# Head norms rewritten by algebra, the MLP's row norm moved to its second product, and a new TensorE order ahead of the attention

## The chip, the cores and the metric

The kernel runs on one core of one Trainium2 chip. The metric is the device time of one execution in microseconds (us), the median of the runs of a kernel. Inside the core the engines run side by side, each through its own list of instructions in order: TensorE (PE, the matmuls), VectorE (DVE), ScalarE (ACT), GpSimd (POOL) and SyncE (SP), which here only issues the transfers (DMA).

## What is computed

Two decoder layers over 256 tokens of 1024 numbers, all in 32-bit floats. The first layer mixes by two attentions (latent attention with compressed queries and keys, and a dilated one); the second by a causal block attention. Each then has a squared-ReLU MLP and a gated input embedding.

```python
def rms_norm(x, g):
    return x * lax.rsqrt(jnp.mean(x * x, axis=-1, keepdims=True) + EPS) * g

for i in range(DEPTH):
    hn = rms_norm(h, mix_norm[i])
    # layer 0: z = hn @ w_in; c_q, c_kv = rms_norm of columns of z (384 and 256 wide);
    #   q = c_q @ w_uq, kv = c_kv @ w_ukv; norms of each head of q and k; rotary parts; attention;
    #   dilated q, k (normed by head), v = other columns of z; attention; both @ w_out
    # layer 1: q, k, v = hn @ w_in; norms of each head of q and k; attention; @ w_out
    h = h + mix
    u = jax.nn.relu(rms_norm(h, ff_norm[i]) @ w_ff1[i])
    h = h + (u * u) @ w_ff2[i]
    g = jax.nn.sigmoid(rms_norm(h, ple_norm[i]) @ w_ple_gate[i])
    h = h + g * (p[i] @ w_ple_proj[i])
```

## The kernel before

**Products in three passes.** Each float32 operand is split into a rounded part `hi` (ACT, line 107) and the rest `lo` (DVE, line 108), and a product is the sum hi·hi + hi·lo + lo·hi. A weight chunk is 1 MB in the big stages and is split in four pieces of 128x512 numbers, so each chunk costs ACT four `hi` and DVE four `lo`. Activations `x` are kept with `hi` and `lo` side by side, so that one matmul of 512 columns (line 233) and one of 256 (line 235) do a chunk's three passes in the MLP.

**Norms.** The gain of a layer's norm is put into `x`; the factor of a row, `rsqrt(mean)`, is applied to a product after the matmul. `Norm.square` sums the squares on ACT and DVE into `acc`; `Norm.rows` (a factor for each token on a partition, two columns) and `Norm.cols` (the same factors along the free axis, 128x256) make TensorE add them over the partitions (tile `st`, lines 195 and 206) and take the root with `rsqrt` (lines 86 to 99): a logarithm and an exponential on ACT and a Newton step of four DVE instructions. `heads_norm` (279), `mla_queries` (680), `mla_keys` (708) and `compress` (646) do the norm of heads and latents with the same `rsqrt`; the squares there wait for the row factor `r`, since the product is scaled by it on the way. The normed tile `z` is then transposed by TensorE (`tr`, line 273).

**MLP.** `up` takes 16 chunks of the first weight: two outputs `f` in the two PSUM banks of pool `pa`, which ACT and DVE add together (lines 490 and 491), DVE clips and multiplies by the row factor (line 492), ACT squares (494) and splits (495, 496). `down` takes 16 chunks of the second weight, and DVE adds the two halves of its product to `h` (507, 508). `cols` of the MLP is called after the first of chunk 0's two outputs.

**What sets the order.** In the stages of attention and projection TensorE's order is that of the code (`manual_schedule`); the very first block, with the combined latent projection (`w_c`, 416 columns in 8 pieces, and `w_kv`), has the order of the code on all engines. Elsewhere, the MLP and the gate included, a scheduler orders the instructions. `take` issues the transfers and splits of weight chunks two chunks ahead. The dense products come in units of six matmuls (`tok_units`), and the attention of four pairs of heads lays units between scores, transposes and values (`attention`, its list `units` saying how many). ACT, DVE and SP take weight splits, norms and softmax in one list each, so a small step waits behind the pieces that stand ahead of it.

## Time and profile before

| | us |
|---|---|
| runs: median of 3 | 697.8 |
| lowest, highest run | 694.3, 698.08 |
| the profiled execution | 692.53 |
| its span (what the profile shows) | 690.5 |
| TensorE busy | 662.8 |
| VectorE busy | 535.4 |
| ScalarE busy | 432.4 |
| GpSimd busy | 7.7 |

The profile shows one execution: for each instruction the engine, the line of the kernel, start and length, and, where an engine stood idle, what released it. `out<-in` are tile names. Matmuls overlap, so the lengths of single ones add up to more than the time that they take: 0.39 us of a 512-column matmul stand 0.23 us apart. A wait stands in brackets behind the instruction that ended it. The granted clock is that of TensorE: 1.00 is its level of 2.4 GHz, and a stretch at 0.50 ran at the lower one, 1.2 GHz.

### The profile page before, as it was taken

To read this page: it belongs to the slowest core of one execution; us is meant where nothing else is said; L and a number is where in the kernel's file an instruction comes from. 1 tells how busy PE (TensorE), PEld (TensorE's weight loads), DVE (VectorE), ACT (ScalarE), POOL (GpSimd) and SP (SyncE) were. 2 spreads that over 40 slices of the span, in tenths; PEclk is the share of its full clock that TensorE was granted. 3 is DMA by queue.
4 is the path that set the end of the run, shared out by engine and by line. 5 is a ranking of instruction groups with operands and counts; after the bars stand their busy time and mean duration, and the time that the engine had idled before them with its cause. 6 is when DMAs were issued, how large, how long until landed. Compare 5 with 4: busy or idle time off the path is not lost.

```text
span 690.5 us, 10700 instructions
## 1 busy us (share of the span) xinstructions
PE 662.8 (96%) x3862; PEld 566.8 (82%) x3862; DVE 535.4 (78%) x1335; ACT 432.4 (63%) x996; POOL 7.7 (1%) x28
## 2 busy tenths in 40 slices
PE   8988999989999999999997999999899999999996
PEld 7776888968888888888876777888788888888885
DVE  5699768688877877879995687666788778787896
ACT  6877786567745647446873676766577465573572
POOL 3100000000000000000000000000000000000000
PEclk9999999999999999999999999999899999999999
DMA  7555433154555555555444443331555655555411
GB/s 231 235 191 181 193 123 123 62 183 158 190 203 183 184 183 183 183 184 183 149 166 173 161 144 137 123 123 61 186 188 193 216 185 192 183 183 187 179 62 61
DMA packets 19492, 114.07 MB, mean 165 GB/s; under 512 B 2288, under 2 KB 5488, under 8 KB 6640
## 3 DMA queue, kind: packets, MB, share of 16 engines
q1 hardware_dynamic: 19440, 113.40, 46.5%
q8 instruction: 30, 0.49, 0.3%
q14 instruction: 22, 0.18, 0.1%
HBM read 112.34 MB, written 1.05 MB: 164 GB/s over the span
## 4 chain that ended last, share of the span: by engine, by line
PE 84%; DVE 6%; ACT 5%; DMA 3%; issue 1%; SPq 1%; POOL 0%; ACTq 0%; DVEq 0%
PE f L233 34%; PE f L235 17%; PE mm L251 12%; PE mm L220 7%; PE g L233 4%; ACT hi L107 3%; PE g L235 2%; DVE lo L108 2%; DMA raw<-w_dil 2%; PE tr L349 1%; PE tr L273 1%; PE s L318 1%; PE o L358 1%; PE s L316 1%; DMA raw<-w_c 1%
## 5 line engine op out<-in xcount | busy, mean ns | idle before, releaser
L107 ACT ACTIVATE hi<-raw 128x512 fp32r<-128x512 f32 (+2 forms) x418 | 237.7, 623 | 121.4 <-PE f L233 82.5
L108 DVE TENSOR_TENSOR lo<-raw,hi 128x512 fp32r<-128x512 f32 (+2 forms) x418 | 270.6, 686 | 37.8 <-ACT hi L107 36.9
L233 PE MATMUL f<-x,hi 128*128 128x512 f32 x512 | 183.8, 403 | 5.8 <-ACT hi L107 5.8
L233 PE MATMUL f<-u,hi 128*128 128x512 f32 x512 | 179.5, 396 | 0.0
L235 PE MATMUL f<-x,lo 128*128 128x256 f32 x512 | 144.7, 283 | 0.0
L235 PE MATMUL f<-u,lo 128*128 128x256 f32 x512 | 142.8, 279 | 0.0
L233 PEld LDWEIGHTS f<-x,hi 128*128 128x128 f32 x512 | 98.1, 192 | 30.2 <-ACT hi L107 6.6
L233 PEld LDWEIGHTS f<-u,hi 128*128 128x128 f32 x512 | 96.1, 188 | 23.1
L251 PE MATMUL mm<-hi,x 128*128 128x512 f32 (+1 forms) x320 | 107.5, 401 | 3.0 <-ACT hi L107 2.4
L235 PEld LDWEIGHTS f<-x,lo 128*128 128x128 f32 x512 | 98.5, 192 | 0.0
L235 PEld LDWEIGHTS f<-u,lo 128*128 128x128 f32 x512 | 96.4, 188 | 0.0
L251 PEld LDWEIGHTS mm<-hi,x 128*128 128x128 f32 x320 | 60.4, 189 | 18.6 <-ACT hi L107 3.8
L251 PE MATMUL mm<-lo,x 128*128 128x512 f32 (+1 forms) x160 | 62.6, 391 | 0.7 <-DVE lo L108 0.5
L494 ACT ACTIVATE sq<-t 128x256 f32<-128x256 f32 x64 | 26.2, 412 | 42.5 <-DVE t L492 42.5
L507 DVE TENSOR_TENSOR h<-f,h 128x256 f32<-128x256 f32 x64 | 26.9, 421 | 32.2 <-PE f L235 32.1
L220 PE MATMUL mm<-x,hi 128*128 128x256 f32 x256 | 48.3, 289 | 0.0
L233 PE MATMUL g<-x,hi 128*128 128x512 f32 x128 | 45.4, 398 | 0.0
L220 PEld LDWEIGHTS mm<-x,hi 128*128 128x128 f32 x256 | 39.5, 190 | 3.7 <-issue 3.4
L496 DVE TENSOR_TENSOR u<-sq,u 128x256 fp32r<-128x256 f32 x64 | 26.7, 420 | 14.9 <-ACT u L495 14.9
L251 PEld LDWEIGHTS mm<-lo,x 128*128 128x128 f32 x160 | 30.5, 191 | 7.0 <-DVE lo L108 2.1
L220 PE MATMUL mm<-x,lo 128*128 128x256 f32 x128 | 36.1, 282 | 0.0
L235 PE MATMUL g<-x,lo 128*128 128x256 f32 x128 | 35.8, 280 | 0.0
(194 smaller groups left out, 784.9 us busy)
## 6 DMA issues: line engine op xcount, KB each, us to landing
raw<-w_f SPq DMA_DIRECT2D x64, 1024.0 KB, 4.7
raw<-w_odd SPq DMA_DIRECT2D x12, 1024.0 KB, 4.7
raw<-w_g SPq DMA_DIRECT2D x8, 1024.0 KB, 4.8
raw<-w_dil SPq DMA_DIRECT2D x6, 1024.0 KB, 4.9
raw<-w_eo SPq DMA_DIRECT2D x4, 1024.0 KB, 4.8
raw<-w_oo SPq DMA_DIRECT2D x4, 1024.0 KB, 4.8
raw<-w_p SPq DMA_DIRECT2D x2, 1024.0 KB, 4.7
raw<-w_c SPq DMA_DIRECT2D x8, 208.0 KB, 3.7
```

The costliest lines, as they stand in the source:

```text
L107: A.activation(hi, src, AF.Copy)
L108: V.tensor_sub(lo, src, hi.bitcast(F32))
L220: T.matmul(ps[:, j, :], lhsT=a[:, kk, j * P:(j + 1) * P], rhs=b[:, k0 + kk, :], start=(done == 0 and kk == 0 and j == 0 and i == 0), stop= ...
L233: T.matmul(ps, lhsT=wh[:, kk, sl], rhs=x[:, kk], start=(first and kk == 0), stop=last, skip_group_check=True)
L235: T.matmul(ps[:, 0, :], lhsT=wl[:, kk, sl], rhs=x[:, kk, 0, :], start=False, stop=last, skip_group_check=True)
L251: T.matmul(pss[t][:, :n], lhsT=a[:, k0 + kk, t * P:(t + 1) * P], rhs=b[:, kk, :], start=(done + kk == 0 and i == 0), stop=(done + kk == to ...
L273: T.transpose(ps[:rows, i, :], s, ident)
L316: T.matmul(s[:, :P], lhsT=qT[:, :P], rhs=kT[:, :P], start=True, stop=True)
L318: T.matmul(s[:, P:], lhsT=qT[:, P:], rhs=kT, start=True, stop=True)
L494: A.activation(sq, t, AF.Square)
L496: V.tensor_sub(ul, sq, uh.bitcast(F32))
L507: V.tensor_add(h[:, k, :], ps[:, 0, :], h[:, k, :])
```

## The change

**Norms of heads.** The squares are taken of the unscaled product, and the row's factor comes in by algebra: with m the mean square of a row plus EPS, a head's factor is the root of the head's mean square plus EPS·m (`e2` is that term). The squares so no longer wait for the root of the row. The small roots (`small_rsqrt`, `row_rsqrt`) go to GpSimd, which now has 119 instructions for 28, the rotary key among them. The steps of a norm are a generator (a "chain") that is advanced by one step with each unit of TensorE's work (`tick`).

**Weights.** A class `Weights` issues the transfer of chunk c + 3 when chunk c is first split, and splits one piece for each unit, the `lo` of a piece behind the `hi` of the next. The gains of the two latent norms are multiplied into `w_uq` and `w_ukv` as these are split, and the latents themselves then need two splits for each half of the tokens.

**MLP.** Relu is positive-homogeneous, so the squared row factor can be applied after the second product: `up` has a Relu on ACT (64 of them) in the place of the DVE instruction of line 492, and `down` has a copy on ACT and three DVE instructions for the two of before. `cols` stands after both outputs of chunk 0.

**Order.** The dilated values are computed ahead of the latent attention, with them 20 units rather than 15, and four units of the dilated keys; in layer 1 the row statistics are asked for ahead of unit 6 instead of after unit 7, and the transposes of queries and keys two units later. Transfers: the first half of `w_kv` is asked for ahead of the last pieces of `w_c`.

```diff
+    def small_rsqrt(y, m):
+        t = sp.tile(list(y.shape), F32, tag=f"nt{list(y.shape)}", name="nt")
+        A.activation(t, m, AF.Ln)
+        A.activation(y, t, AF.Exp, scale=-0.5)
+        G.tensor_mul(t, y, y)
+        G.tensor_mul(t, t, m)
+        G.tensor_scalar(t, t, -0.5, 1.5, op0=OP.mult, op1=OP.add)
+        G.tensor_mul(y, y, t)
+
+    def row_rsqrt(y, ms, n, e2):
+        m = sp.tile(list(y.shape), F32, tag=f"nm{list(y.shape)}", name="nm")
+        G.tensor_scalar_mul(m, ms, 1.0 / n)
+        b = e2 if len(y.shape) == 2 else e2.unsqueeze(2).to_broadcast(list(y.shape))
+        G.tensor_add(m, m, b)
+        small_rsqrt(y, m)
...
+        def piece(self):
...
+            if gain is None:
+                A.activation(hi, raw, AF.Copy)
+                self.flush()
+                self.low = lambda: V.tensor_sub(lo, raw, hi.bitcast(F32))
...
+            if sl.start == 0:
+                self.load(c + 3)
...
+    def tick(n=1):
+        pump(n)
+        for c in list(chains):
+            if next(c, chains) is chains:
+                chains.remove(c)
...
-            r = tp.tile([P, 2], F32, tag="rr", name="rr")
-            rsqrt(r, ps, D)
-            return r
+            e2, m, r = (sp.tile([P, 2], F32, tag=x, name=x) for x in ("e2", "rm", "rr"))
+            V.tensor_scalar(m, ps, 1.0 / D, EPS, op0=OP.mult, op1=OP.add)
+            G.tensor_scalar_mul(e2, m, EPS)
+            small_rsqrt(r, m)
+            return e2, r
...
-            A.activation(sq, pss[t].rearrange("p (a b) -> p a b", a=8), AF.Square,
-                         scale=r[:, t:t + 1])
-            V.tensor_reduce(ms[:, t, :], sq, axis=AX.X, op=OP.add)
-        rs = tp.tile([P, 2, 8], F32, tag="rs", name="rs")
-        rsqrt(rs, ms, 64)
-        V.tensor_mul(rs, rs, r.unsqueeze(2).to_broadcast([P, 2, 8]))
...
+            A.activation(sq, pss[t].rearrange("p (a b) -> p a b", a=8), AF.Square)
+            V.tensor_reduce(ms[:, t, :], sq, axis=AX.X, op=OP.add)
+        yield
+        rs = tp.tile([P, 2, 8], F32, tag="rs", name="rs")
+        row_rsqrt(rs, ms, 64, e2)
+        yield
...
-                    if not rb:
-                        rb.append(n_ff.cols())
...
-                    V.scalar_tensor_tensor(t, t, 0.0, rb[0], op0=OP.max, op1=OP.mult)
+                    A.activation(t, t, AF.Relu)
...
+                if n == 0:
+                    r = n_ff.cols()
+                    A.activation(r, r, AF.Square)
+                    r2.append(r)
...
-                    V.tensor_add(h[:, k, :], ps[:, 0, :], h[:, k, :])
-                    V.tensor_add(h[:, k, :], ps[:, 1, :], h[:, k, :])
+                    t = tp.tile([P, S], F32, tag="z", name="t", bufs=ZB)
+                    A.activation(t, ps[:, 1, :], AF.Copy)
+                    V.tensor_add(t, ps[:, 0, :], t)
+                    V.tensor_mul(t, t, r2[0])
+                    V.tensor_add(h[:, k, :], h[:, k, :], t)
...
+            if k == 5:
+                weights.load(1)
+            if k == 7:
+                weights.load(2)
...
-        attention([mla_pair(j) for j in range(4)], cs[:, C_CAUSAL:C_CAUSAL + 384], None,
-                  mixed, 0, dense, [2, 2, 2, 2, 1])
+        run(dense, 4)
+        attention(mla_pair, cs[:, C_CAUSAL:C_CAUSAL + 384], None, mixed, 0, dense,
+                  [1, 1, 1, 0, 0])
...
+        yield from tok_units(x1, 512, 8, 4, lambda p: start_chain(heads_norm(
+            p, e2[0], q, goq[:, 4 * g:4 * g + 4], bq)), {} if g else {6: [stats1]})
+        yield from tok_units(x1, 512, 8, 4, lambda p: start_chain(heads_norm(
+            p, e2[0], k, vc[:, V_OK:V_OK + 1], bk)), {6: [lambda: bq[0]()]})
```

ScalarE in the head, from the split of the two halves of `w_kv` to the first root, before (lines 107 are weight pieces, 178 and 182 squares of `x`, 576 and 577 the sine tables, 94 and 96 the row's root):

```order
L107 ACTIVATE hi<-raw 128x512 x2
L178 ACTIVATE acc<-h 128x512
L182 ACTIVATE sq<-h 128x512
L107 ACTIVATE hi<-raw 128x512 x2
L182 ACTIVATE sq<-h 128x512 x2
L107 ACTIVATE hi<-raw 128x512 x4
L576 ACTIVATE sn<-ang 128x32
L577 ACTIVATE co<-cang 128x32
L634 ACT_TABLE_LOAD
L94 ACTIVATE nt<-st,eps 128x2
```

and after (177 are weight pieces, 250 and 254 squares of `x`, 713 the squares of the query latent):

```order
L177 ACTIVATE hi<-raw 128x512 x3
L250 ACTIVATE acc<-h 128x512
L177 ACTIVATE hi<-raw 128x512 x2
L254 ACTIVATE sq<-h 128x512
L177 ACTIVATE hi<-raw 128x512 x2
L254 ACTIVATE sq<-h 128x512
L177 ACTIVATE hi<-raw 128x512 x2
L254 ACTIVATE sq<-h 128x512
L177 ACTIVATE hi<-raw 128x512 x2
L713 ACTIVATE sq,cm<-mm 128x384 x2
```

The squares of `x` moved from ahead of the pieces of the dilated weights to between them; six pieces now stand between the first square and the last (one of `w_kv`, four of the first dilated chunk, one of the second), where before all four squares stood ahead of the dilated chunks.

VectorE at the start of the MLP, before (183 the last sum of squares, 95 and 97 to 99 the root of the columns, 491 the sum that empties a PSUM bank of the first product):

```order
L183 TENSOR_TENSOR acc<-acc,sq 128x512
L108 TENSOR_TENSOR lo<-raw,hi 128x512 x5
L95 TENSOR_SCALAR nm<-st 128x256
L97 SCALAR_TENSOR_TENSOR nt<-cr 128x256
L491 TENSOR_TENSOR t<-f_1812,t 128x256
L98 TENSOR_TENSOR nt<-nt,nm 128x256
L491 TENSOR_TENSOR t<-f_1813,t 128x256
```

and after (255 the sum of squares, 566 the emptying of the bank, 92 and 94 the root):

```order
L255 TENSOR_TENSOR acc<-acc,sq 128x512
L179 TENSOR_TENSOR lo<-raw,hi 128x512 x5
L566 TENSOR_TENSOR t<-f_1806,t 128x256
L566 TENSOR_TENSOR t<-f_1807,t 128x256
L92 TENSOR_SCALAR nm<-st 128x256
L94 SCALAR_TENSOR_TENSOR nt<-cr 128x256
```

The emptying of the first bank moved ahead of two steps of the root; the five weight pieces stand ahead of it in both.

VectorE in layer 1, from the last sum of squares to the normed queries `z`, before (95 and 97 to 99 first the row's root, then that of the heads):

```order
L99 SCALAR_TENSOR_TENSOR rr<-nt,rr 128x2
L108 TENSOR_TENSOR lo<-raw,hi 128x512 x2
L288 TENSOR_REDUCE ms<-sq 128x8 x2
L95 TENSOR_SCALAR nm<-ms 128x16
L108 TENSOR_TENSOR lo<-raw,hi 128x512 x2
L97 SCALAR_TENSOR_TENSOR nt<-rs 128x16
L108 TENSOR_TENSOR lo<-raw,hi 128x512
L98 TENSOR_TENSOR nt<-nt,nm 128x16
L108 TENSOR_TENSOR lo<-raw,hi 128x512
L99 SCALAR_TENSOR_TENSOR rs<-nt,rs 128x16
L291 TENSOR_TENSOR rs<-rs,rr 128x16
L294 TENSOR_TENSOR z<-mm,rs 128x512 x2
```

and after (271 the mean of the row, 356 the sums of the heads, 363 the normed queries):

```order
L255 TENSOR_TENSOR acc<-acc,sq 128x512
L179 TENSOR_TENSOR lo<-raw,hi 128x512 x2
L271 TENSOR_SCALAR rm<-st 128x2
L179 TENSOR_TENSOR lo<-raw,hi 128x512 x3
L356 TENSOR_REDUCE ms<-sq 128x8 x2
L179 TENSOR_TENSOR lo<-raw,hi 128x512 x4
L363 TENSOR_TENSOR z<-mm,rs 128x512 x2
```

The steps of the root that stood between weight pieces on VectorE are gone from its list; they are GpSimd's.

## Rows read from the trace of the kernel before

**Rows 1.** The page: span, and each engine's busy time, share and instructions.
```profile
span 690.5 us, 10700 instructions
PE 662.8 (96%) x3862; PEld 566.8 (82%) x3862; DVE 535.4 (78%) x1335; ACT 432.4 (63%) x996; POOL 7.7 (1%) x28
```

**Rows 2.** The waits of TensorE, its three longest: total us, times, longest.
```profile
PE f L233 <- ACT hi L107: 5.8, 2, 2.9
PE tr L273 <- DVE z L294: 4.6, 1, 4.6
PE mm L251 <- DVE rp L698: 3.1, 1, 3.1
```

**Rows 3.** Busy time by stretches: length, each engine, granted clock, DMA share, GB/s.
```profile
30.00:40.00 10.00, 8.85 (x45) 7.40 (x46) 9.55 (x30) 9.99 (x31) 0.00 (x0) 1.00 0.26 80
50.00:60.00 10.00, 8.67 (x34) 6.82 (x35) 10.00 (x41) 7.66 (x17) 0.00 (x0) 0.83 0.59 192
148.00:151.30 3.30, 3.30 (x13) 2.81 (x12) 3.22 (x9) 1.75 (x5) 0.00 (x0) 0.51 0.52 216
160.00:170.00 10.00, 10.00 (x58) 8.65 (x58) 8.86 (x20) 7.49 (x19) 0.00 (x0) 1.00 0.50 195
200.00:210.00 10.00, 10.00 (x58) 8.69 (x57) 7.31 (x15) 3.52 (x7) 0.00 (x0) 1.00 0.48 156
330.00:340.00 10.00, 10.00 (x58) 8.68 (x57) 9.98 (x25) 8.97 (x20) 0.00 (x0) 1.00 0.54 202
369.90:373.40 3.50, 3.50 (x13) 3.11 (x14) 1.89 (x3) 0.00 (x0) 0.00 (x0) 0.51 0.72 281
487.10:492.40 5.30, 5.28 (x17) 4.52 (x18) 4.62 (x11) 1.38 (x5) 0.00 (x0) 0.50 0.62 247
```

**Rows 4.** Timeline, start of the first MLP: start, length, engine, line, operation, wait.
```profile
142.34 3.09 DVE L108 TENSOR_TENSOR lo<-raw,hi 128x512 fp32r<-128x512 f32 x5
145.35 0.42 DVE L95 TENSOR_SCALAR nm<-st 128x256 f32<-128x256 f32 x1
...
146.02 0.42 DVE L491 TENSOR_TENSOR t<-f,t 128x256 f32<-128x256 f32 x1
...
146.58 0.47 PE L233 MATMUL f<-x,hi 128*128 128x512 f32 x1 [2.91 <-ACT hi L107]
```

**Rows 5.** Timeline, the first products of layer 1, TensorE and one sum of squares.
```profile
355.80 0.50 PE L251 MATMUL mm<-hi,x 128*128 128x512 f32 x1 [0.58 <-ACT x L171]
...
358.75 0.95 PE L195 MATMUL st<-ones,acc 128*128 128x1 f32 x8
...
369.86 1.53 PE L273 MATMUL tr<-cs,z 128*128 128x128 f32 x6 [4.56 <-DVE z L294]
...
356.70 0.69 DVE L183 TENSOR_TENSOR acc<-acc,sq 128x512 f32<-128x512 f32 x1
```

**Rows 6.** Timeline, the head: the last piece of `w_c`, and two stops of TensorE.
```profile
14.76 0.55 ACT L107 ACTIVATE hi<-raw 128x416 fp32r<-128x416 f32 x1 [1.72 <-DMA raw<-w_c]
16.03 1.15 ACT L107 ACTIVATE hi<-raw 128x512 fp32r<-128x512 f32 x2 [0.72 <-DMA raw<-w_kv]
...
31.00 0.73 PE L251 MATMUL mm<-hi,x 128*128 128x512 f32 x2 [1.29 <-ACT hi L107]
...
63.67 1.08 PE L273 MATMUL tr<-cs,kf 128*96 128x128 f32 x8 [1.22 <-ACT hi L107]
```

**Rows 7.** Timeline, GpSimd: two additions of one form in the angle tables.
```profile
12.39 0.43 POOL L567 TENSOR_TENSOR ang<-ang,rt 128x32 f32<-128x32 f32 x1
...
14.85 0.25 POOL L567 TENSOR_TENSOR ang<-ang,rt 128x32 f32<-128x32 f32 x1
```

**Rows 8.** Groups by shape, MLP: busy us, mean ns of one, idle before.
```profile
L492 DVE SCALAR_TENSOR_TENSOR t<-t,cr 128x256 f32<-128x256 f32 x64 | 26.8, 421 | 1.0
L490 ACT ACTIVATE t<-f 128x256 f32<-128x256 f32 x64 | 23.7, 373 | 7.1 <-PE f L235 6.6
```

**Rows 9.** Timeline, VectorE: first and last step of one softmax in the latent attention.
```profile
72.45 0.29 DVE L325 CUSTOM_DVE_ANT_0 sc<-s,cs 128x128 f32<-128x128 f32 x1 [2.71 <-PE s L318]
...
74.88 0.55 DVE L340 TENSOR_SCALAR pr<-pr,rd 128x128 f32<-128x128 f32 x2
```

597 lines of the change are left out of this document (325 added, 272 removed).

## The prediction

> **What bounds the kernel now.** The page first: TensorE is busy 662.8 of 690.5 us [rows 1], so nothing on another engine is worth anything except where TensorE waits for it. The stretches come next, since the share is an average: in the MLP TensorE is busy 10.00 of 10.00 us at full clock, beside ACT at 7.49 and VectorE at 8.86 in the first product, 3.52 and 7.31 in the second [rows 3]. A microsecond saved on VectorE there is worth nothing, one added on ACT costs nothing as long as it fits. What can be won is listed among TensorE's waits: 5.8 us in two equal parts at the starts of the two MLPs, 4.6 in front of the transposed queries of layer 1, 3.1 in the latent projections [rows 2], 13.5 us in sum. Then the granted clock: the three stretches behind the first two kinds of wait ran at 0.51, 0.51 and 0.50, and 50 to 60 us, behind the third, at a mean of 0.83 [rows 3]. Half clock over 3.3, 3.5 and 5.3 us gives away up to 1.6, 1.7 and 2.6 us (half of each; less if TensorE would not have been full), and 0.17 of 10 us another 1.7. So the whole prize is some 13.5 + 7.6 = 21 us, and the question is how much of it the change takes and what new waits it makes.
>
> The waits are not what their releasers' names say at the MLP. There the wait is put down to a weight split on ACT, but the matmul that starts at 146.58 needs a PSUM bank, and that comes free when VectorE has read it at 146.02 + 0.42 = 146.44 [rows 4]; VectorE came to it only after five weight pieces (142.34 to 145.35 or so) and two steps of the root, of a pitch of (146.02 − 145.35)/2 = 0.33 us.
>
> **The change part by part.**
>
> *MLP, start.* The order of VectorE shows the five pieces still ahead of the sum that empties the bank, but the two steps of the root behind it. That is 146.02 − 145.35 = 0.67 us earlier [rows 4], for each of two MLPs: **−1.3 us**. What remains is an idle time of about 2.2 us. Idles of 2.9 us (twice), 3.1 and 4.6 were followed by the lower clock [rows 2, 3], one of 1.29 at 31.00 was not (the clock of 30 to 40 us is 1.00) [rows 3, 6]. 2.2 lies between, a little nearer to 2.9; the rest of the pause (the sum over the partitions) is as it was, so I leave the low clock where it is. If it went, 1.6 and 2.6 us more would be won.
>
> *MLP, steady.* `up` loses 64 VectorE instructions of 0.42 us and gains 64 on ACT; `down` gains 64 on each. The page has no Relu; the nearest row on ACT, the copy of the same shape, is 0.37 us [rows 8]. A chunk (two outputs) takes TensorE about 5.5 us, so per 10 us ACT in `up` gets 3.6 x 0.37 = 1.3 more: 7.49 + 1.3 = 8.8, and in the busiest of such stretches somewhat over 9. `down` gets on VectorE 3.6 x 0.42 = 1.5 at most: 7.31 + 1.5 = 8.8. Both fit, beneath a TensorE at 10.00: nothing. Where it does not fit is the last `down` of layer 0 and the gate, with VectorE at 9.98 and ACT at 8.97 already [rows 3]. Four chunks with two more instructions each are up to 8 x 0.42 = 3.4 us; TensorE did not wait there before, so there was slack, and between 0 and 3.4 I take **+0.5 us**, near the end where the row shows TensorE at 10.00.
>
> *Layer 1, queries.* The statistics are now asked for when TensorE has done six units, at the place of the matmul that started at 355.80 after 0.58 us of waiting, so TensorE is there at 355.22. The sum of squares ends at 356.70 + 0.69 = 357.39 [rows 5]. So the wait is 2.2 us instead of 0.58: +1.6. It buys that the root of the rows and the squares of the heads don't follow one another, and that the transposes stand two units later (twelve matmuls of 0.23 us, 2.7 us). The chain after it: the statistics take 0.95 us [rows 5] and units 6 and 7 twelve matmuls of 0.23, so they end at 357.39 + 0.95 + 2.76 = 361.1, and TensorE comes to the transposes six units later, at 361.1 + 8.3 = 369.4. In between lie squares and sums (three steps of about 0.62, the length of a 128x512 instruction [rows 4], the rest side by side), two roots on ACT of some 0.5, six GpSimd steps of 0.25 to 0.43 us [rows 7], the two products that make `z` (1.24), and up to four weight pieces that VectorE's list holds ahead of them (2.5): 361.1 + 1.9 + 0.5 + 1.5 + 1.2 = 366.2 at the earliest, and with 2.6 for GpSimd and all four pieces 369.8. So the wait of 4.56 us [rows 5] goes, with the low clock behind it, of which I count 1.2 of at most 1.7 us since transposes are in it. Sum 1.6 − 4.56 − 1.2: **−4.1 us**. Bounds: +0.4 more if the chain is 0.4 late, +1.0 to +1.7 if the new 2.2 us idle brings the low clock, so −2 to −4.5.
>
> *The head.* Gains: the 3.1 us wait for the rotary part goes, because the projections no longer follow each other through four PSUM banks and one VectorE list [rows 2], and 1.7 of clock behind it [rows 3]; the wait of 1.22 before the transposed keys and 1.29 before the second dilated chunk go too [rows 6]: 7.3 us. Costs: the last piece of `w_c` now stands behind half of `w_kv`; its split began at 14.76 when it had landed, that of `w_kv` at 16.03 [rows 6], so +1.3. The first statistics wait for squares that on ACT stand behind pieces which wait for their own transfers: between nothing and the 3.1 of the longest wait of this stretch; I take 2.3, since the second dilated chunk is late already before (the 1.29). The two latents need a GpSimd chain before their transposes, which in the trace of before were ready: 1.6 (between 0 and six steps at 0.43, 2.6, for the longer one). The attention has fewer units between scores and transposes; one softmax took from 72.45 to 74.88 + 0.55, 3.0 us [rows 9], and behind the last scores there stand now only 2.0 us of matmuls, with up to three weight pieces in VectorE's way: three places of 0.7 each, 2.1. Sum of the costs 7.3: the head comes out at **0 us**, from −7 (none of the new waits) to +4 (each of them at its upper end).
>
> *The rest.* The transfers three chunks ahead rather than two change nothing where no weight was late; the embedding, the dilated attention and the tail keep their order: 0.
>
> Sum: −1.3 + 0.5 − 4.1 + 0 = −4.9 us. The profiled execution would take 692.53 − 4.9 = 687.6; it lies below all three runs shown (median 697.8, lowest 694.3), so the forecast for the median goes by the same difference: 697.8 − 4.9 = **692.9 us**.
>
> **The rivals.**
>
> *All the named waits go.* If the new waits of the head stay near nothing and the clock no longer falls at the MLP starts, the sum is −7 + (−1.3 − 1.6 − 2.6) + 0.5 − 4.1 = −16; half of the head's part gives 697.8 − 12.6 = 685.2. For it: every wait of the list is met by an edit. Against it: the five pieces still stand ahead of the bank.
>
> *GpSimd is slowed by VectorE* (the one on the slower side). The same addition took 0.25 us with VectorE idle and 0.43 beside a VectorE that was working on two operands [rows 7], and VectorE is busy 9.55 and 10.00 of 10 us in the head [rows 3]. A step that waits for a whole weight piece (3.09/5 = 0.62 us [rows 4]) takes 0.87; a chain of six then 5.2 us instead of the 1.5 to 2.6 assumed, some 2.7 to 3.7 more. Four chains have TensorE close behind them (both latents, the dilated queries, those of layer 1): 4 x 3.2 = 12.8 us, less about 1.3 of slack at each of the last three: +8.9, so 692.9 + 8.9 = 701.8 us. It decides from the point at which a step costs over some 0.5 us in these stretches. The Trainium skill (SBUF — State Buffer, section "SBUF: two separate sides") says that GpSimd and a VectorE instruction with two SBUF inputs take a shared pair of ports in turn, the later one standing still for the whole of the other's instruction. This trace agrees as far as the two rows go (0.25 and 0.43); by that rule the time is that of this rival, at worst.
>
> *ACT becomes the bound in `up`.* If the Relu is nearer to 0.6 than to 0.37 or the scheduler's order lets ACT run late, ACT needs 7.49 + 3.6 x 0.6 = 9.7 and in the busiest stretches over 10: with 3% over 177 us of `up` (32 chunks of 5.5), +5 us: 697.9. Against it: the copy at 0.37.
>
> *Little is won.* The new wait in layer 1 brings the low clock (+1.6), the chain ends late (+0.5), the head loses 2: 697.0 us. The change then does what it says, and the waits move.
>
> **How the numbers follow.** Forecast (690 to 695.5) 0.44; all waits go 0.19; little won 0.16; GpSimd slowed 0.13; ACT the bound 0.08. A measurement of this kernel can't tell less than about 0.5%, 3.5 us: under 694.3 is faster, over 701.3 slower. Faster: 0.19 and 0.37 of the forecast, 0.56; slower: GpSimd, 0.13; same: what is left of the forecast, little won and ACT, 0.31. The range leaves out the better half of "all go" (0.09) and the worse part of GpSimd (0.09): 684.5 to 700.
>
> **What would show it.** Right: in layer 1 no wait before the transposes and one of about 2 us for the sum of squares; at the MLP starts an idle of 2.2 rather than 2.9 us; TensorE at 10.00 in the MLP with ACT near 9; in the head no wait of 3 us, but one before the first statistics. Wrong: GpSimd steps at over 0.5 us and transposes that wait for `z`; a TensorE under 10.00 in `up`, waiting for `u` or for a weight piece of a late ACT; low clock in new places.

## The result and the profile after

| | before | after |
|---|---|---|
| median of 12 runs each, us | 693.70 | 696.68 |
| lowest, highest, us | 686.83, 698.08 | 694.18, 702.31 |
| ratio after / before, 95% interval | | 1.0105 [1.0059, 1.0150] |
| the profiled execution, us | 692.53 | 694.22 |
| its span, us | 690.5 | 692.4 |

The changed kernel is slower by 1%; 0.7% faster had been forecast. By stretches of TensorE's own timeline (first matmul of one stage to the first of the next) the two profiled executions differ like this:

| stretch | before, us | after, us | change |
|---|---|---|---|
| start to first `kv` matmul | 17.03 | 19.96 | +2.9 |
| to first dilated product | 6.95 | 7.25 | +0.3 |
| to first scores (15 units of products before, 20 after) | 47.39 | 55.11 | +7.7 |
| to the first MLP (five units fewer after) | 65.01 | 61.74 | -3.3 |
| first MLP, to its gate | 187.04 | 182.89 | -4.2 |
| gate, to the products of layer 1 | 23.47 | 23.23 | -0.2 |
| to the first scores of layer 1 (one unit fewer after) | 45.81 | 42.93 | -2.9 |
| to the embedding (one unit more after) | 44.05 | 47.10 | +3.1 |
| embedding, to the second MLP | 40.18 | 40.17 | 0.0 |
| second MLP, to its gate | 184.82 | 183.10 | -1.7 |
| to the last matmul | 22.94 | 23.12 | +0.2 |

A unit is six matmuls 0.23 us apart, 1.38 us, and five of them are 6.9. So up to the first MLP the head lost 2.9 + 0.3 + (7.7 - 6.9) + (6.9 - 3.3) = 7.6 us. That is the whole loss and more. The eight matmuls of the statistics (0.8 us before, 0.9 after) stand in the second stretch before and in the third after: like for like the second is +1.1, with a granted clock of 0.57 from 20 to 24 us, and the third, without the five units, -0.1.

The page of after, against [rows 1]: span, then busy time, share and instructions.

```profile
span 692.4 us, 10793 instructions
PE 663.7 (96%) x3862; PEld 570.7 (82%) x3862; DVE 526.5 (76%) x1249; ACT 469.4 (68%) x1118; POOL 40.3 (6%) x119
```

VectorE got 9 us lighter, GpSimd 33 busier, and TensorE has as much to wait for as before. Its waits after, against [rows 2]: total us, times, longest.

```profile
PE f L307 <- DVE t L566: 4.3, 2, 2.2
PE st L267 <- DVE acc L255: 3.7, 2, 2.6
PE mm L325 <- DVE lo L179: 2.7, 1, 2.7
PE mm L325 <- ACT hi L122: 2.4, 3, 1.7
PE tr L707 <- DVE ll L123: 2.4, 1, 2.4
```

The three named waits of before are gone or shorter: 5.8 us at the MLP starts became 4.3, the 4.6 of the queries of layer 1 and the 3.1 of the rotary part are gone. Others stand in their place. The clock, against [rows 3]: stretches, busy time of PE, PEld, DVE, ACT, POOL, then the granted clock, DMA share, GB/s.

```profile
43.00:48.00 5.00, 5.00 (x20) 4.56 (x19) 3.65 (x7) 3.01 (x8) 1.10 (x2) 0.66 0.62 210
65.00:69.00 4.00, 3.13 (x18) 2.68 (x19) 4.00 (x8) 2.54 (x6) 0.64 (x2) 1.00 0.27 41
153.00:157.00 4.00, 3.49 (x12) 3.02 (x13) 4.00 (x12) 3.09 (x9) 0.00 (x0) 0.57 1.01 424
200.00:210.00 10.00, 10.00 (x59) 8.82 (x58) 8.95 (x19) 5.15 (x12) 0.00 (x0) 1.00 0.52 199
361.00:369.00 8.00, 7.86 (x24) 6.53 (x25) 4.09 (x9) 2.19 (x6) 2.00 (x5) 0.57 0.70 264
```

The lower clock followed the stops at 18 us (1.7 us long), 42 (2.4), both MLP starts (2.15) and layer 1 (2.6). A mean of 0.57 over 4 us gives away (1 - 0.57) x 4 = 1.7 us. It did not follow the longest, 2.7 us before 65.87. The steady MLP is as forecast: TensorE at 10.00, with VectorE at 8.95 in the second product (8.8 estimated).

**Where the head stands still.** Two pieces of the chain of waits of after: start, length, engine, operation. First up to the transposed key latent at 42.33, then up to a dilated product at 65.87.

```profile
40.64 0.20 POOL kr L106
40.87 0.41 DVE krope L735 x2
41.28 0.53 DVE lo L184
41.81 0.48 DVE ll L123
42.33 0.44 PE tr L707 x2
```

```profile
61.27 0.23 POOL rs L106
61.52 0.42 DVE z L765
...
65.13 0.70 DVE lo L179
65.87 1.42 PE mm L325 x5
```

TensorE's stops are no longer put down to a root but to `ll` and `lo`, ordinary splits; the chain shows what they stood behind. VectorE's list had `krope` and `z` ahead of them, and these waited for GpSimd. VectorE's steps with a POOL wait, from its timeline in the head:

```profile
40.87 0.41 DVE L735 TENSOR_SCALAR krope<-mm,kr 128x32 f32<-128x32 f32 x2 [0.91 <-POOL kr L106]
50.26 1.29 DVE L363 TENSOR_TENSOR z<-mm,rs 128x512 f32<-128x512 f32 x2 [1.00 <-POOL rs L106]
55.87 0.42 DVE L765 TENSOR_TENSOR z<-mm,rs 128x256 f32<-128x256 f32 x1 [0.88 <-POOL rs L106]
61.52 0.42 DVE L765 TENSOR_TENSOR z<-mm,rs 128x256 f32<-128x256 f32 x1 [1.18 <-POOL rs L106]
72.00 1.42 DVE L800 TENSOR_TENSOR kf<-mm,rs 128x256 f32<-128x256 f32 x4 [1.26 <-POOL rs L106]
```

Five stops, 5.2 us, on the engine that in before was busy 9.55 and 10.00 of 10 us there [rows 3].

### The profile page after: what moved, and what is told of

Its sections match the earlier page's. It is cut to its first block, busy times and chain, and to the rows that moved or that the text cites. A ratio compares the mean times of both kernels' runs of the same rounds, so it can differ in the third digit from the quotient of the medians.

```text
span 692.4 us, 10793 instructions
## 1 busy us (share of the span) xinstructions
PE 663.7 (96%) x3862; PEld 570.7 (82%) x3862; DVE 526.5 (76%) x1249; ACT 469.4 (68%) x1118; POOL 40.3 (6%) x119
## 4 chain that ended last, share of the span: by engine, by line
PE 77%; DVE 10%; ACT 5%; POOL 3%; DMA 2%; issue 2%; SPq 1%; DVEq 0%; ACTq 0%
PE f L307 33%; PE f L309 17%; PE mm L325 9%; PE mm L294 6%; PE g L307 4%; DVE lo L179 3%; PE g L309 2%; ACT hi L177 1%; DMA raw<-w_dil 1%; PE tr L414 1%; PE tr L334 1%; DVE x L244 1%; PE o L423 1%; DMA raw<-w_c 1%; DVE acc L255 1%
## 5 line engine op out<-in xcount | busy, mean ns | idle before, releaser
L179 DVE TENSOR_TENSOR lo<-raw,hi 128x512 fp32r<-128x512 f32 (+1 forms) x400 | 269.1, 693 | 62.6 <-ACT hi L177 56.1
L177 ACT ACTIVATE hi<-raw 128x512 fp32r<-128x512 f32 (+1 forms) x400 | 235.4, 626 | 88.7 <-PE f L307 53.8
L307 PE MATMUL f<-x,hi 128*128 128x512 f32 x512 | 181.2, 398 | 4.3 <-DVE t L566 4.3
L325 PE MATMUL mm<-hi,x 128*128 128x512 f32 (+1 forms) x320 | 109.0, 407 | 2.4 <-ACT hi L122 2.4
L325 PEld LDWEIGHTS mm<-hi,x 128*128 128x128 f32 x320 | 62.7, 196 | 16.9 <-ACT hi L122 3.4
L325 PE MATMUL mm<-lo,x 128*128 128x512 f32 (+1 forms) x160 | 64.3, 402 | 3.1 <-DVE lo L179 2.7
L567 ACT ACTIVATE t<-t 128x256 f32<-128x256 f32 x64 | 26.1, 411 | 23.9 <-DVE t L566 23.9
L396 ACT ACTIVATE pr<-sc,nm 128x128 f32<-128x128 f32 x64 | 27.4, 446 | 8.9 <-DVE nm L391 8.9
```

Source lines behind the costliest of these rows:

```text
L177: A.activation(hi, raw, AF.Copy)
L179: self.low = lambda: V.tensor_sub(lo, raw, hi.bitcast(F32))
L307: T.matmul(ps, lhsT=wh[:, kk, sl], rhs=x[:, kk], start=(first and kk == 0), stop=last, skip_group_check=True)
L325: T.matmul(pss[t][:, :n], lhsT=a[:, k0 + kk, t * P:(t + 1) * P], rhs=b[:, kk, :], start=(done + kk == 0 and i == 0), stop=(done + kk == to ...
L396: A.activation(prs[i][:, sl], scs[i][:, sl], AF.Exp, scale=-1.0, bias=nms[i][:, t:t + 1], **kw)
L567: A.activation(t, t, AF.Relu)
```

## The experiments

Ratios are to the kernel before, with 95% intervals; "scores" is the start of the first scores, "layer 1" the stretch from its first product to its first scores (after: 82.3 and 42.93 us). Medians are of 4 to 12 runs; scores, stretches, stops and clock are of one profiled execution each.

### Roots back on VectorE

All steps of the small roots in the changed kernel on VectorE, nothing else.

```diff
-        G.tensor_mul(t, y, y)
-        G.tensor_mul(t, t, m)
-        G.tensor_scalar(t, t, -0.5, 1.5, op0=OP.mult, op1=OP.add)
-        G.tensor_mul(y, y, t)
+        V.tensor_mul(t, y, y)
+        V.tensor_mul(t, t, m)
+        V.tensor_scalar(t, t, -0.5, 1.5, op0=OP.mult, op1=OP.add)
+        V.tensor_mul(y, y, t)
```

> The changed kernel with the small roots, and the terms they need, on VectorE instead of GpSimd; order, gains, MLP and rotary key as changed. GpSimd theory (the chains are slow there, 0.19 to 0.64 us a step and later at up to 1.4 us for two, and ACT, VectorE and TensorE wait for them in turn): the scores of the latent attention begin 2 us or more earlier than the 82.3 to 83.8 us of the runs with that head, the idle times that VectorE and ACT spend on GpSimd's roots (1.0 us six times before z, 1.2 before the latent's copies) go, and the whole is 2 to 4 us faster than the changed kernel. Order theory (what stands ahead in ACT's and VectorE's lists decides): the steps now wait behind weight pieces on VectorE, the scores move by less than 1 us.

Measured: 688.07 us, 0.9936 [0.9899, 0.9973], 8.6 us under after by the medians; scores at 76.6. The stretch from the first dilated product to the scores went from 55.11 to 49.26 us (-5.9), the attention of layer 1 from 47.1 to 45.9. TensorE's waits in this head, up to 85 us (total, times, longest):

```profile
PE mm L325 <- ACT hi L122: 2.8, 2, 1.7
...
PE st L267 <- DVE acc L255: 0.9, 1, 0.9
...
PE tr L707 <- DVE ll L123: 0.2, 1, 0.2
```

The wait of 2.4 for `ll` is 0.2, that of 2.7 for `lo` is gone, and so is the half clock of 43 to 48 us. VectorE's timeline there shows how: the root of the dilated queries takes longer than on GpSimd (from the end of the sums at 44.05 to `z` at 48.73, 4.7 us; in after from 46.49 to 50.26, 3.8), but weight pieces and other sums fill the gaps:

```profile
46.79 0.17 DVE L103 TENSOR_TENSOR nt<-rs 128x16 f32<-128x16 f32 x1
46.88 0.28 DVE L753 TENSOR_REDUCE ms<-sq 128x4 f32<-128x128 f32 x1
...
47.30 0.17 DVE L105 TENSOR_SCALAR nt<-nt 128x16 f32<-128x16 f32 x1
47.38 0.69 DVE L179 TENSOR_TENSOR lo<-raw,hi 128x512 fp32r<-128x512 f32 x1
47.98 0.17 DVE L106 TENSOR_TENSOR rs<-rs,nt 128x16 f32<-128x16 f32 x1
```

So in this order the roots on GpSimd cost some 6 us of the head. It is more than one execution's chance: in the eight profiled executions of this section that have the changed order of units and the roots on GpSimd, after included, scores start at 81.7 to 83.8 us, in the three with the roots on VectorE at 76.6 to 79.0. It isn't the length of the chain that costs: VectorE does other work while its own chain runs, and in after it stands at `z` until GpSimd is done. Whether a later place for `z` in VectorE's list would do as well was not tried.

### GpSimd's steps alone, in the kernel before

The last steps of the small roots on GpSimd, in the old order of everything (the mean stays on VectorE).

```diff
+        if E is G:
+            G.tensor_mul(t, y, y)
+            G.tensor_mul(t, t, m)
+            G.tensor_scalar(t, t, -0.5, 1.5, op0=OP.mult, op1=OP.add)
+            G.tensor_mul(y, y, t)
+            return
```

> The kernel before, with one part of the change alone: the last steps of the small roots (four instructions on GpSimd for three on VectorE, everything but the 128x256 row factor; the mean stays on VectorE); the order of the units, the norms and the splits are those of before. Theory (a root on GpSimd costs by itself, since VectorE's next product stands in its list and waits for it, 0.9 to 1.3 us each of five times in the head of the changed kernel): the head gets longer by 3 to 6 us (first scores at 74 to 77 us instead of 71.4), the wait before the transposed queries of layer 1 grows from 4.6 to 5.5 us or more, ratio 1.004 to 1.012. Rival (GpSimd's roots cost only in the new order, where the transposes are close behind them): first scores at 71 to 72.5 us and a ratio of 0.997 to 1.003.

Measured: 692.10 us, 0.9971 [0.9936, 1.0006]; scores at 72.0 (before 71.4). The rival was right: on their own the steps cost nothing that can be measured. VectorE waits for them here just as long, 5.6 us in six waits ahead of the scores, against 5.2 in five in after; two of the six:

```profile
43.04 0.18 DVE L298 TENSOR_TENSOR rs<-rs,rr 128x16 f32<-128x16 f32 x1 [1.37 <-POOL rs L102]
...
56.91 0.42 DVE L702 TENSOR_TENSOR z<-mm,rs 128x256 f32<-128x256 f32 x1 [1.01 <-POOL rs L102]
```

But TensorE's stops up to 80 us sum to 7.3 us, in before to 8.8; the stretch ahead of the scores got 1.8 us longer by a half clock from 50 to 58 us, twice as long as before. In layer 1 the wait before the queries even fell:

```profile
366.66 1.32 PE L280 MATMUL tr<-cs,z 128*128 128x128 f32 x8 [2.68 <-DVE z L301]
```

against 4.56 in [rows 5]: no weight piece stands between the steps of the root any more. So VectorE's waits are not a price by themselves. What costs is the combination: roots on GpSimd in the head as the change rewrites it. Which part of that rewriting (the chains, the weight plan, the splits of the latents) leaves TensorE no slack behind VectorE's waits was not separated.

### The order of units ahead of the attention

The changed kernel with the units, weight plan and transposes ahead of the attention in the order of before.

```diff
-        dil_v = tok_units(x0, 512, 8, 4, lambda p: values(p, r0[0], dv),
-                          {2: [lambda: bdq[0]()], 6: [lambda: bq0[0]()]})
-        run(dil_v, 4)
...
+            yield from tok_units(x0, 512, 8, 4, lambda p: values(p, r0[0], dv),
+                                 {4: [lambda: bdk[0]()]})
```

> The changed kernel with the order ahead of the first attention undone: dilated values and keys woven into the latent attention again (7 units ahead, 2, 2, 2, 2, 1 within), with all norms, gains and GpSimd roots as changed. Order theory: the stretch from the first scores to the MLP, 61.7 us where the order of before took 65.0 with five units of 1.4 us more in it, falls by 3 to 4 us for like work, and the first product of the MLP starts at 140 to 141 us instead of 144 to 145.5. Rival (the norms by GpSimd are the loss, wherever the units stand): VectorE and TensorE stop for roots between the projections again, by 3 us or more, and the MLP starts at 143.5 us or later.

Measured: 700.14 us, 1.0105 [1.0046, 1.0165]. With the same 15 units ahead of them as in before, scores start at 77.3 against 71.4, and the waits for `rp` (2.9) and `ll` (2.4) are there; 3.7 us of the 5.9 stand ahead of the first `kv` matmul, where no unit was moved. The first MLP starts at 146.5, as the rival had it (143.5 or later). Undoing the order of the units wins nothing; it is not the cause by itself.

### Three suspects in the head that were not it

**Sine tables and table load** behind the first `kv` pieces, instead of ahead of the last split of `x`:

```diff
-            if k == 6:
-                tabq, tabk = rope_tables(*angles)
-                A.preload_act_table_set(LN_EXP)
...
+            if k == 0:
+                tabq, tabk = rope_tables(*angles)
+                A.preload_act_table_set(LN_EXP)
```

> The changed kernel with one part undone: the sine tables and the load of ACT's second table stand behind the first weight pieces of w_kv again instead of ahead of the last piece of x. Order theory (the last split of x, its data landed at 14.78, started at 17.28 because sines and table load stood ahead of it on ACT): TensorE's stop of 1.71 us before the last product of w_c shrinks to under 0.8 us, w_kv starts at 18.0 to 18.5 us instead of 19.96, and the first statistics 1 to 2 us earlier. Rival (the transfers bound this stretch: the last piece of w_c landed at 15.36, the first dilated chunk at 23.7): w_kv starts earlier but TensorE then stops longer for the statistics, whose squares stand behind the dilated pieces, and the first statistics move by less than 0.5 us.

Measured: 697.13 us, 1.0086 [1.0044, 1.0129]. The first `kv` matmul comes at 17.6 (after 20.0), but the statistics only at 29.3 (29.9) and the scores at 81.7: the gain goes into stops of 1.0 and 1.4 us ahead of them, with half clock from 26 to 37 us. The rival was nearly right.

**The low parts of a split at once**, not behind the next high part:

```diff
-                self.flush()
-                self.low = lambda: V.tensor_sub(lo, raw, hi.bitcast(F32))
+                V.tensor_sub(lo, raw, hi.bitcast(F32))
```

> The changed kernel with each lo piece issued with its own hi piece instead of behind the next one. Deferral theory: the stop of 2.7 to 3.1 us near 63 us, where TensorE waits for a lo whose hi had been ready for some 8 us, goes, and the scores of the latent attention begin 2.5 us earlier than the 82.3 to 83.8 of the runs with that head. Rival (VectorE's list is late there whatever the place of the lo, since the rotary parts of the second queries wait for GpSimd and run 3 us): the stop moves to another instruction and the scores by less than 1 us.

Measured: 695.17 us, 1.0044 [1.0002, 1.0086]. The stop for `lo` is gone, but scores are at 82.2: it moved to `ll` (2.8), `mk` (1.4) and `dq` (0.8), as the rival had it.

**The rotary key's chain three units later**, out of the way of `ll`:

```diff
-                       3: [lambda: start_chain(rotary_key(pss, e2, krope, krr))],
-                       6: [lambda: cq[0]()], 7: [lambda: ck[0]()]}))
+                       6: [lambda: start_chain(rotary_key(pss, e2, krope, krr)), lambda: cq[0]()],
+                       7: [lambda: ck[0]()]}))
```

> The changed kernel with the rotary key's chain started at unit 6 of the dilated queries instead of unit 3. Queue theory: on VectorE the scaling of the rotary key waited for GpSimd (0.91 us idle at 39.96 to 40.87) with the latent's lo parts queued behind it, and TensorE stopped 2.38 us for these; with the chain later, VectorE reaches the lo parts 1 us or more earlier, the stop falls under 1 us and the scores of the latent attention begin 1 to 2 us earlier than the 82.3 to 83.8 us of the runs with that head. Rival (the latent's own chain is what is late): the stop stays at 2 us or more, and the scores don't move by 0.5 us.

Measured: 697.73 us, 1.0095 [1.0062, 1.0127]; the stop at the key latent fell from 2.4 to 1.9, scores at 82.9. In these three runs taking one stop away moved the scores by less than 1 us.

### Layer 1: the statistics

In after TensorE asks for them before the sum of squares is there. ScalarE, then VectorE and TensorE, from the timeline of after (compare [rows 5]):

```profile
357.64 1.28 ACT L948 ACT_TABLE_LOAD   x1
358.94 0.91 ACT L243 ACTIVATE x<-h,vc 128x256 fp32r<-128x256 f32 x2
...
360.40 0.69 DVE L255 TENSOR_TENSOR acc<-acc,sq 128x512 f32<-128x512 f32 x1
...
361.14 1.71 PE L267 MATMUL st<-ones,acc 128*128 128x1 f32 x8 [2.61 <-DVE acc L255]
```

Asked for behind unit 7 instead, in the changed kernel:

```diff
+        def q_done(p):
+            if not e2:
+                stats1()
+            start_chain(heads_norm(p, e2[0], q, goq[:, 4 * g:4 * g + 4], bq))
...
-            p, e2[0], q, goq[:, 4 * g:4 * g + 4], bq)), {} if g else {6: [stats1]})
```

> The changed kernel with one part undone: in layer 1 the row statistics are asked for after unit 7 of the queries again, not ahead of unit 6. Order theory (the stop of 2.61 us before the statistics and the half clock behind it, 361.1 to 367.7 us, ate what the removed stop of 4.56 us gave): the stop shrinks to under 1 us, the half clock behind it goes, and the stretch from the first product of layer 1 to the first scores (42.9 us in the changed kernel, 42.9 + 1.4 in the order of before) loses 3 to 5 us; the transposes, reached with 1.7 us in hand in the changed kernel, still don't wait. Rival (the roots on GpSimd are too slow to be started later): a stop of 1 us or more comes up before the transposes and the stretch gains less than 1.5 us.

Measured: 696.51 us, 1.0064 [1.0027, 1.0101]; layer 1 takes 38.83 us (-4.1), with no half clock; a stop of 1.5 us for a split of `x` is left. The gain forecast for this stage was there to be had, two units later. Most of the 4.1 us is the clock. The run with chunk 0 in other banks (below) leaves this stage as in after and has the same stop of 2.61 us, but no half clock followed it:

```profile
363.40:371.40 8.00, 7.88 (x39) 6.71 (x40) 6.92 (x13) 4.39 (x11) 3.50 (x8) 1.00 0.69 264
```

There layer 1 takes 39.72 us: 3.2 of the 4.1 us are the half clock, 0.9 the stop.

In after the table load, which the scheduler put ahead of the last splits of `x`, stands within that wait. Put behind the last square (statistics ahead of unit 6, as in after):

```diff
-        pre = tc.keep_in_program_order(A.preload_act_table_set(LN_EXP))
+        with tc.issue_after(n1.last.ins):
+            pre = tc.keep_in_program_order(A.preload_act_table_set(LN_EXP))
```

> The changed kernel with one thing set: in layer 1 the load of ACT's table (1.28 us) comes after the last square, as it came in the kernel before, and not ahead of the last two splits of x. The statistics stay ahead of unit 6. Table theory: the sum of squares ends 1.3 us earlier and the stop before the statistics goes from 2.61 to about 1.3 us; a stop of 1.3 us left the clock at 1.00 elsewhere, so the half clock behind it goes too, and 3 to 4 us are won up to the first scores. Rival: the half clock comes with the shorter stop as well, and 1.3 us are won.

Measured: 697.73 us, 1.0114 [1.0068, 1.0159]; layer 1 takes 41.22 us (-1.7), but the wait is as long as before:

```profile
366.01 1.35 PE L267 MATMUL st<-ones,acc 128*128 128x1 f32 x8 [2.51 <-DVE acc L255]
```

The load did move behind the square; ScalarE put two more weight pieces in its place, so that the splits of `x` came 0.4 us earlier and the sum of squares 0.1. The 1.7 us are a half clock half as long (0.79 over the 8 us from the statistics, in after 0.57). The run with the rotary key's chain later, which leaves layer 1 as in after, had the same 0.79 by itself, and 41.35 us. Neither the theory nor the rival holds: the place of the load alone is not shown to count. With late statistics as well it gives 0.6 us (38.83 to 38.23, in the kernels with the parts together).

### The MLP

The MLP part alone, put into the kernel before (Relu on ScalarE, the squared factor behind the second product, `cols` behind both outputs):

```diff
-                    V.scalar_tensor_tensor(t, t, 0.0, rb[0], op0=OP.max, op1=OP.mult)
+                    A.activation(t, t, AF.Relu)
```

> The kernel before with only the MLP part of the change (row factor squared on the second product, Relu on ACT, cols after chunk 0). Both theories: head and layer 1 as in the kernel before (first scores 71.4, MLP at 136.4 us). If the MLP part is a gain: the stops at the MLP starts are 2.2 instead of 2.9 us, the stretch of the second MLP is 0.7 to 2.5 us shorter, and the whole 1 to 4 us faster than before. If ACT's 128 further instructions cost: a TensorE under full in the MLP, waits for u or lo pieces there, and the whole not faster than before.

Measured: 690.61 us, 0.9971 [0.9937, 1.0006]; stops of 2.2 us at the MLP starts, as in after. This part is the same or a little better; it does no harm. The second MLP, forecast shorter, took 186.3 us against 184.8, by the slower of the two paces told of at the end.

The first outputs of each MLP in four free banks of pool `pm`, first for chunk 0 alone, in the changed kernel:

```diff
-                pss = [pa.tile([P, 2, S], F32, tag="s", name="f1") for _ in range(2)]
+                pool, tag = (pm, "mm") if n == 0 else (pa, "s")
+                pss = [pool.tile([P, 2, S], F32, tag=tag, name="f1") for _ in range(2)]
```

> The changed kernel with the first chunk of each MLP in two banks of the other PSUM pool, so that the second chunk finds free banks and need not wait for VectorE to empty the first. Bank theory: the stops of 2.15 us at both MLP starts go, and with them the half clock behind them; from the first product of the MLP to its middle 3 to 4.5 us are won in each of the two layers, 6 to 9 us in all. Rival (the weight pieces of the second chunk, five of them still to be split on VectorE, are late as well): TensorE stops for a lo piece instead, and less than 1 us is won in each.

Measured: 694.31 us, 1.0053 [1.0023, 1.0084]. The stop only came one chunk later (2.28 us at 159.29), when VectorE was no further on; in this execution no half clock followed it, nor the one of the second MLP (2.27).

Then for the first two chunks, in the kernel before, with the transposes of layer 1 at unit 6 instead of 4:

```diff
-        late = {4: [lambda: fin.pop()()]}
+        late = {6: [lambda: fin.pop()()]}
```

> The kernel before with two small edits and none of the change: the first two chunks of each MLP use the four banks of the other PSUM pool, and the transposes of layer 1 stand two units later. If the stops named in the trace of before can be met one by one: the stops of 2.9 us at both MLP starts go (TensorE goes on in other banks while VectorE works off its list; with one chunk in them the stop only moved one chunk on), the stop of 4.56 us in layer 1 shrinks to under 2, and the whole is 6 to 12 us faster than before, the half clock behind these stops included. Rival (VectorE's backlog, five weight pieces and a root, shows up somewhere anyway): the stops move on again and less than 3 us is won.

Measured: 683.81 us, 0.9866 [0.9821, 0.9911]. Two small moves in the kernel before bring more than the change was forecast to, but not as the expectation had it. The wait of 4.6 is 1.8. The stops at the MLP starts did not go: they came later (2.2 us at 156.99 and 492.83), with a clock of 0.57 over 4 us at each, as the rival had it. In the profiled execution layer 1 is 2.7 us shorter, the MLPs 1.5 and 2.4. With the MLP part on top:

> The kernel before with the four banks for the first two chunks of each MLP, the transposes of layer 1 two units later, and the MLP part of the change. If the MLP part is a gain of its own (less work on VectorE at the start of the MLP): 1 to 3 us faster than the same kernel without it (683.8 us, 1.3% under before). If ACT's instructions cost what VectorE wins: within 1 us of it.

Measured: 683.75 us, 0.9849 [0.9770, 0.9928]. The medians are the same, but with four runs each the interval is wider than the 1 to 3 us that were asked for, so this does not decide.

### The parts together

The changed kernel with late statistics, table load behind the square, late sine tables and two chunks in free banks, roots still on GpSimd:

> The changed kernel with four places mended together: layer 1's statistics after unit 7, ACT's table there after the last square, the head's tables behind the first weight pieces, and four banks for the first two chunks of each MLP. If the losses found one by one add up: layer 1 up to its scores 3 to 5 us shorter than 42.9, the head 1 to 2 us, the MLPs 2 to 5 us; the whole 5 to 10 us faster than the changed kernel, so within 1% of the kernel before or up to 0.5% faster. If they hide one another (one random low-clock stretch in the place of another): less than 3 us.

Measured: 686.98 us, 0.9932 [0.9897, 0.9966]; layer 1 38.23 us, but scores at 83.0: the stages behind the head are mended (9.7 us under after by the medians, as much as expected), the head is not. The same with the roots on VectorE:

> The changed kernel with all that the experiments point to: small roots back on VectorE, the statistics of layer 1 behind unit 7, its table load behind the last square, the sine tables behind the first kv pieces, the first two chunks of each MLP in the free banks. Theory (the parts add up): first scores at 76 to 77 us, as with the roots on VectorE alone, and the stages behind as in the kernel with the other mends (38.2 us from the first product of layer 1 to its first scores; MLPs 173 to 181): span 677 to 681, median 677 to 682, ratio 0.976 to 0.984. Rival (the head's gain is lost again to other stops, VectorE being the fuller engine there): first scores at 79 us or later, ratio 0.987 or above, no better than the kernel before with the free banks.

Measured: 685.43 us, 0.9894 [0.9852, 0.9936]; scores at 79.0, not 76.6: the rival was right. The late sine tables were the next suspect; the same kernel with early ones:

> As e14_vector_mended, but the sine tables and the table load stand where the change put them. Theory (late tables gain 2.4 us at the first kv matmul and lose it and more by a stop at the first statistics that half clock follows, 28 to 35 us in two runs with late tables and in none with early ones): first scores at 76 to 77.5 us instead of 79.0, span 679 to 681, median 680 to 684, ratio 0.982 to 0.987. Rival (the half clock there is chance): first scores at 79 us again or with the clock lost in another place, ratio 0.988 to 0.992.

Measured: 683.89 us, 0.9848 [0.9802, 0.9894]; scores at 77.1 though the first `kv` matmul came 3.9 us later. The stretch from the first dilated product to the scores takes 48.9 us here and 54.1 with late tables; the windows of the two (late first, columns as above):

```profile
28.00:35.00 7.00, 5.46 (x18) 4.53 (x18) 6.72 (x22) 6.02 (x20) 0.00 (x0) 0.51 0.46 139
```

```profile
28.00:35.00 7.00, 6.45 (x34) 5.20 (x33) 6.80 (x20) 6.57 (x21) 0.00 (x0) 1.00 0.45 146
```

In these two executions the TensorE that starts earlier stops for its pieces (1.1, 1.4 and 1.5 us) and pays by the clock. That early tables prevent this is not shown: with them and the roots on GpSimd two executions had half clock behind the statistics as well (statistics late in layer 1, a stop of 2.67 us, and chunk 0 in other banks, 1.99), and the intervals of the two medians overlap. By the medians this kernel beats before by 1.5% and after by 1.8%, and it is level with the two above (683.8).

## Why the prediction was wrong

**The head, forecast at 0, was +7.6.** Three terms were off, one by far.
- *The products up to the scores*: the gains of 7.3 less 2.3 for the statistics and 1.6 for the latents' GpSimd chains make -3.4; measured +0.8, of which 0.9 are the matmuls of the statistics that moved in here. With the roots on VectorE it is 49.26 - 6.9 - 47.39 = -5.0. So the waits that were to go went, the other terms were right or too dear, and the step that failed is "1.6 for the GpSimd chains": it was 5.9, with 1.7 of half clock (43 to 48 us) in it. I had counted chains that TensorE waits for directly, and two of them. The price lies where VectorE waits for GpSimd, five times, with splits queued behind that TensorE needs at once; in the old order VectorE waited as long (5.6 us) and TensorE did not.
- *The start*: 1.3 forecast for the transfer that stands later, 2.9 measured. With the tables late it is 17.55 - 17.03 = 0.5, so the transfer costs less than forecast and the rest is ScalarE's order. ACT's list has the sine tables (which wait 0.94 us for GpSimd) and the table load ahead of the last split of `x`:

```profile
15.74 0.23 ACT L660 ACTIVATE co<-cang 128x32 f32<-128x32 f32 x1 [0.94 <-POOL cang L657]
15.99 1.28 ACT L846 ACT_TABLE_LOAD   x1
17.28 0.51 ACT L243 ACTIVATE x<-h,vc 128x256 fp32r<-128x256 f32 x1
```

  I had not priced this. In the end little hung on it: in the runs without it, TensorE stopped later.
- *The attention*: 2.1 forecast, 6.9 - 3.3 = 3.6 measured. Its stretch is 61.7 to 61.8 us with roots on either engine. TensorE's stops before the softmax's transposes sum to 2.3 us, in before there are none, and with the units of before put back there are none at that place (one of 2.4 us comes up elsewhere): so the priced waits were about right. The other 1.3 us are in no stop: five units fewer freed 5.6 us there and not 6.9, and why stays open.

**GpSimd slowed by VectorE, given 0.13, was the nearest of the rivals, for half of its reason.** From the GpSimd timeline, the chain of the dilated queries and that of the first latent queries:

```profile
46.58 0.64 POOL L111 TENSOR_SCALAR nm<-ms 128x16 f32<-128x16 f32 x1 [3.78 <-DVE ms L356]
47.30 0.46 POOL L113 TENSOR_TENSOR nm<-nm,e 128x16 f32<-128x16 f32 x1
48.72 0.61 POOL L103 TENSOR_TENSOR nt<-rs 128x16 f32<-128x16 f32 x1 [0.95 <-ACT rs L102]
49.41 0.22 POOL L104 TENSOR_TENSOR nt<-nt,nm 128x16 f32<-128x16 f32 x1
...
54.72 0.21 POOL L103 TENSOR_TENSOR nt<-rs 128x16 f32<-128x16 f32 x1 [0.81 <-ACT rs L102]
```

In these rows a step beside a `lo` piece of VectorE takes 0.46 to 0.64 us, one by itself 0.2, and the one at 54.72, beside a VectorE sum with one SBUF operand (from 54.57, 0.42 us long), 0.21. Over the 76 steps of the roots the mean is 0.48 us for the 32 that overlap a VectorE instruction and 0.21 for the 44 that don't. This agrees with the Trainium skill (SBUF — State Buffer, section "SBUF: two separate sides"): a VectorE instruction with two SBUF inputs and a GpSimd instruction exclude one another. But the mean stays under the 0.5 us from which the rival decides, and two of the chains with a VectorE stop behind them (55.87 and 61.52) ran their last four steps at 0.2. The lost time came by the stop itself; how much of the 5.9 us is the slower steps was not separated. "Little is won", given 0.16, had named the lower clock behind the new wait in layer 1, which came; its 697.0 us lies next to the measured 696.7 only by the base, since it stands for 0.8 us won and 3.0 were lost.

**Layer 1, forecast at -4.1, was +0.2** (-2.9 + 3.1). The wait of 4.56 went, as forecast: `z` was ready 1.7 us before TensorE came to it. The wait for the statistics was 2.61 (2.2 forecast). What failed is the clock: I had counted 1.2 us won behind the old wait, and the new one was followed by 0.57 over 8 us, 3.4 us against 1.7 before. I had priced that only as a bound of 1.0 to 1.7. That it is the clock, the run with chunk 0 in other banks shows: the same stop, no half clock, 3.2 us less. Another 1.0 us is a longer wait for `x` before a transpose in the attention (1.3, before 0.3).

**The MLP starts were right:** forecast 0.67 earlier and 2.2 of idle, measured 2.15 each, by the very step named (five pieces, then the sum that empties the bank), against [rows 4]:

```profile
150.03 3.09 DVE L179 TENSOR_TENSOR lo<-raw,hi 128x512 fp32r<-128x512 f32 x5
...
153.04 0.75 DVE L566 TENSOR_TENSOR t<-f,t 128x256 f32<-128x256 f32 x2
...
153.51 0.80 PE L307 MATMUL f<-x,hi 128*128 128x512 f32 x1 [2.15 <-DVE t L566]
```

The lower clock stayed, as forecast, but behind the second start half as long as before (0.83 over 489 to 499 us, before 0.66 over 484 to 494), which is 1.7 us. The steady MLP was 0 for 0.5, and ScalarE never the bound. In all the MLPs came out 4.2 + 1.7 = 5.9 us shorter where 0.8 was forecast: by luck, since the 1.7 of clock and the 3.4 of pace told of below are in no term. They hide part of what the head and layer 1 lost.

**The level** was off too: the forecast took the median of the first three runs, 697.8, as its base, and over 12 runs it is 693.7. That the measured 696.7 lies within the stated 684.5 to 700 is owed to this base; moved by it, the range would be 680.4 to 695.9.

## What to carry to other kernels

Moving small steps from a busy engine to an idle one frees less than it seems to where the busy engine's next instruction in its list needs the result: look for what is queued behind that instruction and who waits for it. Such steps cost some 6 us here in the new order and nothing that could be measured in the old. Where TensorE is nearly full, a wait that is taken away came back at a later place in several of these runs, so mends had to be made together, and a stop can cost by the lower clock behind it as well. Before moving a request earlier, ask when its input is there: the two units by which the statistics came too early cost 0.9 us, and 3.2 more where the clock fell. Read the wait itself after an edit, and not the stage's time alone: the table load seemed to win 1.7 us that were the clock's.

## What the hardware showed unexpectedly

**Two paces of one MLP.** Each MLP of the 17 profiled executions runs, in both its products and at a granted clock of 1.00, at one of two paces. In 100 us of the first and of the second MLP before, and of the first after, whose second reads the same (length, busy time and matmuls of TensorE, clock, DMA share, GB/s):

```profile
200.00:300.00 100.00, 100.00 (x568) 1.00 0.52 184
530.00:630.00 100.00, 100.00 (x579) 1.00 0.55 195
```

```profile
200.00:300.00 100.00, 100.00 (x579) 1.00 0.54 191
```

A pair of matmuls (512 and 256 columns) stands 353 or 347 ns apart, which is 3.4 us in an MLP. The pace is not the change's: kernels with the same MLP code showed both, and in the one profiled run of the roots on VectorE both MLPs were slow (568 each). So 3.4 of the 4.2 us by which the first MLP got shorter are this, and without it the two executions would differ by 1.9 + 3.4 = 5.3 us. What chooses the pace stays open.

**The lower clock is not bound to a stop's length alone.** In one execution of after the clock fell behind stops of 1.7 to 2.6 us and stayed at 1.00 behind one of 2.7 (65 to 69 us in the windows above). The stop of 2.2 us in the MLP was followed by 0.57 in after, and by 1.00 (150 to 165 us) a chunk later in the run with chunk 0 in other banks. The stop before the statistics of layer 1 (2.5 to 2.6 us, in eight executions with early statistics) was followed over 8 us by a mean of 0.57 in five, 0.79 in two and 1.00 in one, and the stage took 42.9 to 43.0, 41.2 to 41.4 and 39.7 us. So the clock's share of a forecast is a spread, not a price.
